# Second attention: seven of eighteen key tiles in float32, the other eleven split from PSUM, and row maxima of two heads at a time

## Chip, cores and metric

The kernel runs on one core of a Trainium2 chip. The metric is the device time of one execution in microseconds (us), median of three runs.

## What is computed

Two transformer blocks run one after the other on 2048 tokens of width 1024. The first has latent attention and a state space part. The second has attention with shared keys beside retention, then a mixture of 32 experts. Only the attention of the second block is touched. Cut to what matters it is

```python
def _attend(q, k, v):          # q (2048, 8 heads, 64); k, v (256 + 2048 keys, 2 heads, 64)
    scale = HEAD_DIM ** -0.5
    def one_block(q_blk):      # 128 queries; four query heads share a key head
        s = jnp.einsum('bqhgd,bkhd->bhgqk', q_blk, k) * scale
        p = jax.nn.softmax(s, axis=-1)
        return jnp.einsum('bhgqk,bkhd->bqhgd', p, v)
```

All inputs and outputs are float32. There are 2304 keys, 18 tiles of 128.

## The kernel before

The program is written with a framework that adds the waits and that may also shift an instruction ahead of others on its engine where operands are late. The source order is the order of first preference. Every large product uses operands of the type `float32r` (R in the code), the high and low parts of a split number; a plain float32 operand is F.

`phase_b` (L1630) makes projections. For each tile of tokens its `do_kv` (L1710) writes the keys' high and low parts to memory (k.k2), and splits the values in two: ACT casts (L318), DVE subtracts (L319), and SP stores the pair in k.v2 (L1719).

`Attention2` (L1092) works in 32 units, each of 128 queries of the four heads that share keys. `run` (L1270) is one loop over 32 x 18 steps, one key tile per step, and the parts of neighbouring units overlap in it:

- `load_q` (L1141) loads the queries of the next unit on SP's queue: q (high and low parts of a head on 128 partitions, L1146), and qm (the high parts and room for one row, L1148).
- `top` (L1151) finds the row maxima of the next unit: for each head five products pa of 512 (the last 256) keys on PE (L1161), each followed by a maximum on DVE (L1162). A last maximum (L1165), four transposes and an ACT scaling (L1173) put the negatives in row 64 of qm. The tuple `TOP` says how many of these pieces are taken in each of the 18 steps; what is left over is taken at the start of the next unit.
- `scores` (L1176): two products (L1182, L1183) give the scores of a tile less the maximum, keys on partitions, in one of two PSUM banks of the pool pS.
- `exps` (L1185): ACT takes the exponential into SBUF (p, L1187) and casts it to its high part (ph, L1191).
- `rest` (L1193): the low part pl = p - ph, on DVE for even tiles and on POOL for odd ones (L1199). High parts of the odd tiles below 17 are added up on DVE (accD, L1209); `fold` (L1214) splits the sum (L318, L319).
- `values` (L1223), five steps later: o += both parts of the values times ph (L1232); o1 += (ones, high parts of the values) times pl (L1234, L1238); and for the tiles marked E, and for the two parts of the folded sum, a product with one column of ones (L1236).
- `finish` (L1240) reads o and o1, divides by the sums and stores.
- At the steps `SIDE` (1, 9, 11, 15) one piece of retention is put in (L970 to L1087). Each takes a PSUM bank from `bank()`, of which there are two, and leaves one to some ten instructions on PE, DVE, ACT and POOL. Within a step, ACT, the maxima and the subtractions come in this order:

```python
            if n < N:
                self.exps(us[n], t)
            for _ in range(self.TOP[t]):
                next(ahead, None)
            if 0 < i <= N * NK:
                self.rest(us[(i - 1) // NK], (i - 1) % NK)
            if t in self.SIDE:
                next(self.side, None)
```

PSUM's eight banks are pA 2 (pa), pS 2 (scores), pO 2 (o, o1), pT 2.

Of the kernel before, what the change touches and what calls it, by code (L numbers as in the profile page):

```python
# [10 lines left out]
F = mybir.dt.float32  # L11
R = mybir.dt.float32r
# [3 lines left out]
OP = mybir.AluOpType  # L16
# [17 lines left out]
class K:  # L34
    """What every part of the kernel shares: the core, the arguments, constants, small helpers."""
# [27 lines left out]
    def tr(self, out, x):  # L63
        """out = x transposed, bit for bit."""
        self.nc.tensor.transpose(out, x, self.ident)  # L65

    def rsqrt(self, out, src, n):
        """out = (src / n + eps) ** -0.5 on small tiles."""
        nc = self.nc
        nc.vector.tensor_scalar(out, src, 1.0 / n, EPS, op0=OP.mult, op1=OP.add)  # L70
        w = out.free_size()
        nc.gpsimd.tensor_tensor(out, out, self.mhalf[: out.partition_size(), :w], op=OP.pow)  # L72

    def reduce_angle(self, x, k):
        """x -> x - 2 pi round(x / 2 pi), within [-pi, pi]; k: room of x's shape."""
# [8 lines left out]
    def sin_cos(self, pool, s, c, x, shape):  # L84
        """s, c = sin(x), cos(x); x is spent."""
# [8 lines left out]
    def cmul(self, pool, ore, oim, are, aim, bre, bim, shape, neg_im=False, second=None):  # L94
        """(ore + i oim) = a b, elementwise; with neg_im, oim = -Im(a b)."""
# [16 lines left out]
# Chunks of 16 tokens. Lanes of the tables: (direction, state). A table of powers has 17 entries e:  # L112
# lambda^e forward, lambda^(16 - e) backward.
# [3 lines left out]
def early(k):  # L117
    """What rests on the parameters alone, in small parts."""
# [56 lines left out]
        # Powers 0..16, ascending for both directions: [lanes, e, g].  # L175
# [16 lines left out]
        # Bbar = (lambda_bar - 1) / lambda B  # L192
# [18 lines left out]
        # Tables with e in the direction's order; pw: lambda^s' forward, lambda^(15 - s') backward.  # L211
# [10 lines left out]
        # Bbar with columns (direction, h), zero off its direction.  # L222
# [10 lines left out]
        # The skip weights, on the diagonal of lag 0: rows 32 j + h of a batch of two groups.  # L233
# [72 lines left out]
def mm3(nc, out, lh, ll, rh, rl, start, stop):  # L306
    """out (+)= (lh + ll)^T (rh + rl) in three passes; the product of the low parts is below float32."""
# [5 lines left out]
def split(nc, hi, lo, src, eng=None):  # L313
    """src = hi + lo exactly, each of 12 bits."""
# [13 lines left out]
class Proj:  # L328
    """Rows of a normalized matrix, transposed and split, against weights that stream through."""
# [18 lines left out]
    def half_block(self):  # L348
        """Room of up to two tiles, in that of the last block's low parts."""
# [4 lines left out]
    def add_rows(self, blk, i, x):  # L354
        """Tile i of four of a block: x [128 rows, 1024]."""
# [8 lines left out]
    def weights(self, c0, n, w=None, upto=8):  # L364
        """Columns of the weights, split; w: the rows that are there already."""
# [12 lines left out]
    def rows(self, blk, i, w, n):  # L378
        """PSUM [128 rows of tile i, n]."""
# [6 lines left out]
    def cols(self, blk, w, m):  # L386
        """PSUM [128 columns of weight tile m, 512 rows]."""
# [7 lines left out]
def norm_rows(k, pool, out, x, g, n, b=None):  # L395
    """out = x / rms(x) * g (+ b) over n columns."""
# [73 lines left out]
def rope_tables_1(k):  # L470
    """[c, s, (cos, cos)] and [c, s, (-sin, sin)] of 32 frequencies, to memory. Yields after each small part."""
# [140 lines left out]
class Attention:  # L612
    """For each head and 128 queries: scores with the queries on partitions, their maximum, the
    exponentials, their transposes split in two; for 256 queries the products with the values
    (stationary). The parts of neighbouring tiles of queries alternate as `order` says."""
# [25 lines left out]
    def start(self, n):  # L641
        """The tile n of queries and what it holds."""
# [20 lines left out]
    def M(self, t, j):  # L663
        """The scores times -scale, in place, and the running minimum."""
# [43 lines left out]
    def D(self, t, g, copy=None):  # L708
        """A group that stays whole, for products in float32."""
# [6 lines left out]
    def Y(self, t, g):  # L716
        """Split from the copy: the high part here, the low part on the engine that has time."""
# [6 lines left out]
    def P(self, b):  # L724
        """A share of a block's products with the values."""
# [22 lines left out]
    def X(self, b):  # L748
        """One over the sums, on all partitions."""
# [39 lines left out]
class Attention1(Attention):  # L789
# [11 lines left out]
        # The next phase's loads go to the room of the even heads, which is free first.  # L801
# [9 lines left out]
    def load_part(self, h, c):  # L811
        """One of eight parts of a head's keys and values, if it isn't there yet."""
# [87 lines left out]
        # log of the decays: -log(1 + exp(-x)), as min(x, 0) - log(1 + exp(-|x|)).  # L900
# [12 lines left out]
        # Distances on partitions: p + 1, 128 - p, 127 - p, p; and 255 - p, 127 - p, p, 128 + p.  # L913
# [5 lines left out]
        # Factors [128, head, direction]: of the queries; of the keys, with 1/8; of the context's keys.  # L919
# [7 lines left out]
        # Over a chunk, on the state's partitions (direction, dk).  # L927
# [4 lines left out]
        # Decays of the scores [key j, head, query i], with 1/8.  # L932
# [20 lines left out]
class Retention:  # L953
    def constants(self, k, cp):
        """Tables of the decays."""
        self.k = k
        k.rsb = k.scratch("rsb", [NT, 64, 512])        # states of the backward direction before each chunk
        k.ruf = k.scratch("ruf", [NT, 64, 512])        # what each chunk adds to the forward state
# [3 lines left out]
    def spread(self, wk, x, j, name):  # L962
        """[row, head, direction, 64]: x [row, (head, 64)] times factor j."""
# [128 lines left out]
class Attention2:  # L1092
# [92 lines left out]
    def exps(self, u, t):  # L1185
# [4 lines left out]
        if self.HI[t] == "A":  # L1190
            self.nc.scalar.copy(hi, p)  # L1191
# [1287 lines left out]
```

## Time and profile before

| | |
|---|---|
| median of 3 runs | 4474.56 us (4474.19 to 4477.1) |
| profiled execution, first to last instruction (span) | 4460.7 us |
| mean granted TensorE clock | 0.962 |
| second attention, first to last score product (L1183) | 2130.1 to 3185.6 us, 32 units |

The page gives no other time of the profiled execution than its span; the median of the runs is 13.9 us above it. In the profile, PE is the matmul engine and PEld its weight loads, DVE, ACT and POOL the vector, scalar and GpSimd engines, SP the queue that issues most transfers. The end of a matmul's record is modelled, and records of neighbouring matmuls overlap; what a matmul costs in a stream is read from the distance of starts. A float32 (F) matmul leaves two records, a float32r matmul one.

### The profile page before, as it was taken

The page shows a single profiled execution, that of the slowest core. Times are in us where ns is not written, and L with a number is a line of the kernel's source. Part 1 is how long each engine was busy: PE and PEld are TensorE (multiplying, and loading weights), DVE is VectorE, ACT ScalarE, POOL GpSimd, SP SyncE. Part 2 cuts the span into 40 slices and gives each one's busy share as a digit, 9 for nine tenths or more (in the row PEclk, how much of TensorE's full clock was granted, in tenths as well). Part 3 has the DMA queues.
Part 4 walks back from the last instruction along what each step waited for, and adds up shares of the span by engine and source line. Part 5 has one row for each costly group of instructions (what it writes and reads, how often), then busy time and mean ns, then how long its engine had stood idle before and what let it go on. Part 6 is the DMA issues. An engine that isn't in the chain of part 4 may idle for free. (4 is left out here: it accounts for less than half of the span.)

```text
span 4460.7 us, 60030 instructions
## 1 busy us (share of the span) xinstructions
PE 4063.1 (91%) x19842; PEld 3214.7 (72%) x19842; DVE 3244.0 (73%) x5326; ACT 2301.0 (52%) x4166; POOL 1988.3 (45%) x2239
## 2 busy tenths in 40 slices
PE   7999889999988989999888888989898799999997
PEld 5777768888876878887666666666587677777775
DVE  7563368887625365534999999999765778888886
ACT  3233455555524343322667777777521556666664
POOL 3430078882003422222555555555300566666664
PEclk9999989999998999999999999999999899999998
DMA  5543852331253464334421111110352788888885
GB/s 142 169 146 109 280 192 74 92 112 53 66 160 123 132 206 127 121 103 135 117 71 52 50 45 43 50 41 25 96 172 95 265 279 280 284 280 275 277 282 184
DMA packets 432999, 647.63 MB, mean 145 GB/s; under 512 B 88576, under 2 KB 228096, under 8 KB 432428
## 3 DMA queue, kind: packets, MB, share of 16 engines
q1 hardware_dynamic: 403868, 562.67, 39.9%
q0 software_dynamic: 21840, 66.25, 4.2%
q10 hardware_dynamic: 6976, 14.85, 1.0%
q8 instruction: 157, 2.57, 0.2%
q14 instruction: 158, 1.29, 0.1%
HBM read 496.33 MB, written 156.10 MB: 146 GB/s over the span
## 5 line engine op out<-in xcount | busy, mean ns | idle before, releaser
L1199 POOL TENSOR_TENSOR pl<-p,ph 128x512 fp32r<-128x512 f32 x288 | 416.1, 1450 | 244.8 <-ACT ph L1191 189.4
L2251 DVE TENSOR_TENSOR wlo<-raw,whi 128x1024 fp32r<-128x1024 f32 x256 | 471.6, 1855 | 66.1 <-ACT whi L2248 66.0
L2248 ACT CAST whi<-raw 128x1024 fp32r<-128x1024 f32 x384 | 394.9, 1048 | 130.9 <-DMA raw<-in_moe_w_up 43.9
L1162 DVE TENSOR_REDUCE nm<-pa 128x1 f32<-128x512 f32 (+1 forms) x640 | 390.0, 623 | 19.7 <-PE pa L1161 18.4
L1187 ACT ACTIVATE p<-ps 128x512 f32<-128x512 f32 x576 | 333.2, 599 | 105.6 <-PE ps L1183 87.0
L1161 PE MATMUL pa<-kk,q 128*128 128x512 f32 (+1 forms) x640 | 266.3, 425 | 95.7 <-DVE nm L1162 85.1
L1191 ACT CAST ph<-p 128x512 fp32r<-128x512 f32 x576 | 342.6, 624 | 7.7
L2251 POOL TENSOR_TENSOR wlo<-raw,whi 128x1024 fp32r<-128x1024 f32 x128 | 319.6, 2504 | 53.5 <-ACT whi L2248 47.4
L310 PE MATMUL z<-wh,hlo 128*128 128x512 f32 (+2 forms) x816 | 304.7, 374 | 0.0
L308 PE MATMUL z<-wh,hhi 128*128 128x512 f32 (+2 forms) x768 | 291.4, 381 | 7.5 <-DVE zo L455 2.4
L309 PE MATMUL z<-wl,hhi 128*128 128x512 f32 (+2 forms) x768 | 289.4, 377 | 2.7 <-DVE wl L319 2.7
L72 POOL TENSOR_TENSOR nr<-nr,mhalf 128x1 f32<-128x1 f32 x98 | 61.7, 631 | 499.2 <-DVE nr L70 441.1
L1199 DVE TENSOR_TENSOR pl<-p,ph 128x512 fp32r<-128x512 f32 x288 | 275.4, 956 | 9.8 <-ACT ph L1191 8.3
L1161 PEld LDWEIGHTS pa<-kk,q 128*128 128x128 f32 x640 | 124.0, 195 | 198.4 <-DVE nm L1162 167.0
L1182 PE MATMUL ps<-q,kk 128*128 128x512 f32 x576 | 241.5, 420 | 0.3
L661 PE MATMUL s<-kn,q 128*128 128x512 f32 x768 | 230.0, 407 | 10.0 <-ACT p L674 5.7
L1238 PE MATMUL o<-pl,v 128*128 128x512 f32 x544 | 220.4, 409 | 17.3 <-DVE pl L1199 12.6
L1232 PE MATMUL o<-ph,v 128*128 128x512 f32 x576 | 233.0, 407 | 2.7 <-DVE oc L1249 2.5
L1183 PE MATMUL ps<-qm,kl 65*128 65x512 f32 x576 | 229.0, 407 | 0.2
L1209 DVE TENSOR_TENSOR accD<-accD,ph 128x512 f32<-128x512 f32 x192 | 224.7, 1170 | 0.3
L693 ACT CAST ph<-pt 128x512 fp32r<-128x512 f32 x256 | 142.8, 596 | 151.1 <-PE pt L65 147.8
L697 DVE TENSOR_TENSOR pl<-pt,ph 128x512 fp32r<-128x512 f32 x256 | 167.9, 685 | 67.4 <-ACT ph L693 66.8
(634 smaller groups left out, 11924.5 us busy)
## 6 DMA issues: line engine op xcount, KB each, us to landing
raw<-in_moe_w_gate SPq DMA_DIRECT2D x128, 512.0 KB
raw<-in_moe_w_up SPq DMA_DIRECT2D x128, 512.0 KB
raw<-in_moe_w_down SPq DMA_DIRECT2D x128, 512.0 KB
raw<-in_w_in SPq DMA_DIRECT2D x136, 256.0 KB
w<-in_w_ada SPq DMA_DIRECT2D x96, 256.0 KB
xt<-in_x SPq DMA_DIRECT2D x32, 512.0 KB
xt<-x SPq DMA_DIRECT2D x28, 512.0 KB
rv<-rv SPq DMA_DIRECT2D x34, 256.0 KB
```

The lines of the kernel that those rows point to most:

```text
L308: nc.tensor.matmul(out, lh, rh, start=start, stop=False)
L309: nc.tensor.matmul(out, lh, rl, start=False, stop=False)
L310: return nc.tensor.matmul(out, ll, rh, start=False, stop=stop)
L1161: nc.tensor.matmul(pa[:, :c1 - c0], q[:, h], kk[:, c0:c1], start=True, stop=True)
L1162: nc.vector.tensor_reduce(nm[:, h, c:c + 1], pa[:, :c1 - c0], axis=AX.X, op=OP.max)
L1182: nc.tensor.matmul(ps, kk[:, ts], q, start=True, stop=False)
L1187: self.nc.scalar.activation(p, u["s"].pop(t), AF.Exp, scale=self.scale)
L1191: self.nc.scalar.copy(hi, p)
L1199: (nc.vector if self.LO[t] == "D" else nc.gpsimd).tensor_tensor(lo, p, hi.bitcast(F), op=OP.subtract)
L1232: nc.tensor.matmul(u["o"], v[:, t, 64:], hi, start=first, stop=last)
L2248: nc.scalar.copy(hi, raw)
L2251: i = eng.tensor_tensor(lo, raw, hi.bitcast(F), op=OP.subtract)
```

## The change

The 18 key tiles of the second attention are put in two lists. For the seven in WHOLE2 the exponentials stay float32 (p in SBUF) and are multiplied, as one float32 matmul, with float32 (ones, values). For the eleven in SPLIT2 the exponential is written back over the scores in PSUM, ACT casts its high part from there, and DVE alone subtracts there. POOL adds up the high parts of all eleven; one float32 matmul with a matrix whose first column is one adds that sum to o1. The products with a column of ones, `fold` and its split are gone.

The maxima come from the queries' high parts alone (before, high plus low) times the keys' high parts: two heads at a time, the one on rows 0 to 63 of the array, the other on rows 64 to 127, in two banks, then two maxima. Their queries are a third copy, qt, loaded by two more transfers. `TOP` holds 13 pieces where there are 12 (before 21 where there were 22). The score banks are three instead of two, the transposes' bank is one instead of two.

```diff
+WHOLE2 = (2, 4, 7, 9, 12, 14, 17)
+SPLIT2 = tuple(t for t in range(NT + 2) if t not in WHOLE2)
...
-    TOP = (1, 1, 1, 1, 2, 1, 1, 1, 2, 1, 1, 1, 2, 1, 1, 1, 1, 1)
+    TOP = (1, 0, 1, 1, 0, 1, 1, 0, 1, 1, 0, 1, 1, 0, 1, 1, 1, 1)
-    LO = "DPDPDPDPDPDPDPDPDP"
-    ACC = "EDEDEDEDEDEDEDEDEE"
...
-        self.pS = ctx.enter_context(k.pool("a2s", 2, space=PSUM))
+        self.pS = ctx.enter_context(k.pool("a2s", 3, space=PSUM))
-        self.pT = ctx.enter_context(k.pool("a2t", 2, space=PSUM))
+        self.pT = ctx.enter_context(k.pool("a2t", 1, space=PSUM))
-        self.ones = cp.tile([128, 1], R, name="on1")
-        nc.vector.tensor_copy(self.ones, k.ones[:, 0:1])
+        self.one = cp.tile([128, 128], F, name="on1")
+        nc.vector.memset(self.one, 0.0)
+        nc.vector.memset(self.one[:, 0:1], 1.0)
...
-            v = cp.tile([128, self.NK, 192], R, name=f"v{g}")
+            v = cp.tile([128, len(SPLIT2), 192], R, name=f"v{g}")
+            vw = cp.tile([128, len(WHOLE2), 128], F, name=f"vw{g}")
...
+            nc.sync.dma_start(vw[:, :, 64:], k.v2w[g].rearrange("t p n -> p t n"))
...
     def load_q(self, n):
...
+        qt = self.qp.tile([128, 2, 128], R, name="qt")
+        for i in range(2):
+            self.nc.sync.dma_start(qt[64 * i:64 * i + 64].bitcast(F), src[0:64, i::2])
...
     def top(self, n):
-        for h in range(4):
+        for j in range(2):
             for c in range(5):
                 c0, c1 = c * 512, min(c * 512 + 512, self.NK * 128)
-                pa = self.pA.tile([128, 512], F, name="pa")
-                nc.tensor.matmul(pa[:, :c1 - c0], q[:, h], kk[:, c0:c1], start=True, stop=True)
-                nc.vector.tensor_reduce(nm[:, h, c:c + 1], pa[:, :c1 - c0], axis=AX.X, op=OP.max)
+                pa = [self.pA.tile([128, 512], F, name="pa") for _ in range(2)]
+                for i in range(2):
+                    r = slice(64 * i, 64 * i + 64)
+                    nc.tensor.matmul(pa[i][:, :c1 - c0], qt[r, j], kk[r, c0:c1], start=True, stop=True)
+                for i in range(2):
+                    nc.vector.tensor_reduce(nm[:, 2 * j + i, c:c + 1], pa[i][:, :c1 - c0], axis=AX.X, op=OP.max)
                 yield
...
     def exps(self, u, t):
+        ps = u["s"].pop(t)
+        if t in WHOLE2:
+            u["p"][t] = p = self.wk.tile([128, 512], F, name="p", bufs=5)
+            self.nc.scalar.activation(p, ps, AF.Exp, scale=self.scale)
+            return
+        self.nc.scalar.activation(ps, ps, AF.Exp, scale=self.scale)
+        hi = self.wk.tile([128, 512], R, name="ph", bufs=self.RING)
+        self.nc.scalar.copy(hi, ps)
...
     def rest(self, u, t):
+        if t in WHOLE2:
+            return
         lo = self.wk.tile([128, 512], R, name="pl", bufs=self.RING)
-        (nc.vector if self.LO[t] == "D" else nc.gpsimd).tensor_tensor(lo, p, hi.bitcast(F), op=OP.subtract)
+        nc.vector.tensor_tensor(lo, ps, hi.bitcast(F), op=OP.subtract)
...
+            nc.gpsimd.tensor_tensor(acc, u["acc"], hi.bitcast(F), op=OP.add)
...
     def values(self, u, t):
-        for x in ([hi] if self.ACC[t] == "E" else []) + (u["sum"] if last and "sum" in u else []):
-            nc.tensor.matmul(u["o1"][0:1], self.ones, x, start=False, stop=False)
+        if last:
+            nc.tensor.matmul(u["o1"], self.one, u["acc"], start=False, stop=False)
+        if t in WHOLE2:
+            nc.tensor.matmul(u["o1"], vw[:, WHOLE2.index(t)], p, start=False, stop=last)
+        else:
+            nc.tensor.matmul(u["o"], v[:, j, 64:], hi, start=first, stop=t == SPLIT2[-1])
+            nc.tensor.matmul(u["o1"], v[:, j, 0:128], lo, start=first, stop=last)
...
         def do_kv(z, s):
+            if kt in WHOLE2:
+                vw = wk.tile([128, 2, 64], F, name="vt")
+                nc.scalar.copy(vw, v)
+                nc.sync.dma_start(k.v2w[:, WHOLE2.index(kt)].rearrange("h p n -> p h n"), vw)
```

## Rows read from the trace of the kernel before

**Rows 1.** The page's engines: busy time, share of the span, instructions

```profile
PE 4063.1 (91%) x19842; PEld 3214.7 (72%) x19842; DVE 3244.0 (73%) x5326; ACT 2301.0 (52%) x4166; POOL 1988.3 (45%) x2239
```

**Rows 2.** Windows of first attention, projections, second attention: length, engines, clock, DMA

```profile
core 0: us, PE busy (x) PEld busy (x) DVE busy (x) ACT busy (x) POOL busy (x), PEclk, DMA share, GB/s
640.00:1250.00 610.00, 603.80 (x3778) 520.53 (x3777) 486.26 (x1061) 330.09 (x828) 352.09 (x866) 1.00 0.26 77
1620.00:2108.00 488.00, 471.38 (x2401) 390.39 (x2402) 248.35 (x505) 166.81 (x338) 107.70 (x166) 0.99 0.41 130
2143.00:3151.00 1008.00, 897.84 (x3969) 627.74 (x3968) 985.30 (x1583) 735.57 (x1371) 561.67 (x393) 0.97 0.19 51
```

**Rows 3.** Waits in 2143 to 3150 us: us in total, times, longest

```profile
PEld pa L1161 <- DVE nm L1162: 155.1, 195, 4.2
PE pa L1161 <- DVE nm L1162: 81.2, 87, 3.8
PE pa L1161 <- DMA q<-q: 3.9, 7, 1.7
```

**Rows 4.** Line L1183, weight loads and matmuls: ns min/median/max, first and last start

```profile
L1183 PEld LDWEIGHTS ps<-qm,kl x576: 186/188/334, 2130.0 to 3185.4; 65*128 65x128 f32 x192
L1183 PE MATMUL ps<-qm,kl x576: 387/396/774, 2130.1 to 3185.6; 65*128 65x512 f32 x192
```

**Rows 5.** Instruction groups of DVE and ACT in 2143 to 3150 us

```profile
L1162 DVE TENSOR_REDUCE nm<-pa 128x1 f32<-128x512 f32 x483 | 325.0, 676 | 10.7 <-PE pa L1161 10.1
L1191 ACT CAST ph<-p 128x512 fp32r<-128x512 f32 x545 | 324.6, 624 | 7.5
L1187 ACT ACTIVATE p<-ps 128x512 f32<-128x512 f32 x544 | 314.7, 599 | 93.0 <-PE ps L1183 77.2 <-POOL pl L1199 8.0 <-PE pa L1161 2.4
L1199 DVE TENSOR_TENSOR pl<-p,ph 128x512 fp32r<-128x512 f32 x272 | 256.8, 944 | 7.8 <-ACT ph L1191 6.5
L1209 DVE TENSOR_TENSOR accD<-accD,ph 128x512 f32<-128x512 f32 x181 | 208.6, 1153 | 0.3
L1076 DVE TENSOR_SCALAR on<-on,mv,r 128x128 f32<-128x128 f32 x64 | 51.2, 850 | 1.6 <-POOL r L72 1.6
L1162 DVE TENSOR_REDUCE nm<-pa 128x1 f32<-128x256 f32 x120 | 49.0, 408 | 0.3
L1209 DVE TENSOR_TENSOR accD<-ph 128x512 f32<-128x512 f32 x30 | 31.7, 1056 | 0.0
L319 DVE TENSOR_TENSOR suml<-accD,sumh 128x512 fp32r<-128x512 f32 x30 | 21.1, 703 | 0.0
L319 DVE TENSOR_TENSOR wol<-raw,woh 128x1024 fp32r<-128x1024 f32 x1 | 1.2, 1212 | 0.0
```

**Rows 6.** Timeline of PE, second attention: start us, length of the record

```profile
2166.28 0.40 PE L1236 MATMUL o<-ph,on 128*1 128x512 f32 x1
2166.51 0.40 PE L1236 MATMUL o<-sumh,on 128*1 128x512 f32 x1
...
2167.69 0.52 PE L1161 MATMUL pa<-kk,q 128*128 128x256 f32 x2
2168.05 0.39 PE L1182 MATMUL ps<-q,kk 128*128 128x512 f32 x1
```

**Rows 7.** Timeline of a retention piece on PE; two instruction groups of retention

```profile
2610.02 0.39 PE L1060 MATMUL pt<-rv,sm 128*128 128x128 f32 x2
2610.24 0.39 PE L1061 MATMUL pt<-rst,qxt 128*128 128x128 f32 x2
...
L1061 PE MATMUL pt<-rst,qxt 128*128 128x128 f32 x128 | 24.7, 274 | 0.0
L65 PE MATMUL pt<-ident,on 128*128 128x128 f32 x64 | 12.9, 304 | 1.6 <-DVE on L1076 1.6
```

**Rows 8.** Subtractions of the two attentions by line: ns min/median/max, first and last start

```profile
L697 DVE TENSOR_TENSOR pl<-pt,ph x256: 671/683/693, 643.0 to 1259.0; 128x512 fp32r<-128x512 f32 x128
L1199 DVE TENSOR_TENSOR pl<-p,ph x288: 669/692/2964, 2133.5 to 3187.2; 128x512 fp32r<-128x512 f32 x144
L1199 POOL TENSOR_TENSOR pl<-p,ph x288: 1253/1314/2086, 2137.5 to 3188.3; 128x512 fp32r<-128x512 f32 x144
```

**Rows 9.** Float32 matmuls: timeline of PE (256 columns), line L1569 (512 columns)

```profile
1259.08 1.03 PE L1394 MATMUL pz<-tz,ut 128*128 128x256 f32 x4
1259.95 0.59 PE L1396 MATMUL pz<-o,st 128*128 128x256 f32 x2
...
L1569 PE MATMUL pz<-acc,ones x32: 590/590/591, 681.0 to 1101.3; 128*1 128x512 f32 x32
```

**Rows 10.** Timeline of loads and of PE where a unit begins

```profile
2596.47 0.55 SPq L1146 DMA_DIRECT2D q<-q  x1
2597.10 0.60 SPq L1148 DMA_DIRECT2D qm<-q  x1
...
2599.69 0.79 PE L1161 MATMUL pa<-kk,q 128*128 128x512 f32 x1 [0.39 <-DMA q<-q]
```

More of the change, by code (lines that the diff above doesn't have):

```diff
@@ L1134, in __init__ @@
             nc.sync.dma_start(v[:, :, 64:].bitcast(F), k.v2[g].rearrange("t p n -> p t n"))
-            nc.gpsimd.tensor_copy(v[:, :, 0:64], k.ones[:, None, 0:64].to_broadcast([128, self.NK, 64]))
-            self.kv.append((kk, kl, v))
+            nc.sync.dma_start(vw[:, :, 64:], k.v2w[g].rearrange("t p n -> p t n"))
+            nc.gpsimd.tensor_copy(v[:, :, 0:64], k.ones[:, None, 0:64].to_broadcast([128, len(SPLIT2), 64]))
+            nc.gpsimd.tensor_copy(vw[:, :, 0:64], k.ones[:, None, 0:64].to_broadcast([128, len(WHOLE2), 64]))
+            self.kv.append((kk, kl, v, vw))
     def bank(self):
@@ L1178, in scores @@
         kk, kl = self.kv[u["n"] % 2][:2]
-        q, qm = (x.rearrange("p h n -> p (h n)") for x in self.q[u["n"]])
+        q, qm = (x.rearrange("p h n -> p (h n)") for x in self.q[u["n"]][:2])
         ts = slice(t * 128, t * 128 + 128)
@@ L1185, in exps @@
     def exps(self, u, t):
-        p = self.wk.tile([128, 512], F, name="p", bufs=5)
-        self.nc.scalar.activation(p, u["s"].pop(t), AF.Exp, scale=self.scale)
+        ps = u["s"].pop(t)
[4 more added lines that the diff above has]
+        self.nc.scalar.activation(ps, ps, AF.Exp, scale=self.scale)
         hi = self.wk.tile([128, 512], R, name="ph", bufs=self.RING)
-        u["p"][t] = [p, hi]
-        if self.HI[t] == "A":
-            self.nc.scalar.copy(hi, p)
+        self.nc.scalar.copy(hi, ps)
+        u["p"][t] = ps, hi
     def rest(self, u, t):
         nc = self.nc
-        p, hi = u["p"][t]
-        if self.HI[t] == "D":
-            nc.vector.tensor_copy(hi, p)
+        if t in WHOLE2:
+            return
+        ps, hi = u["p"][t]
         lo = self.wk.tile([128, 512], R, name="pl", bufs=self.RING)
-        (nc.vector if self.LO[t] == "D" else nc.gpsimd).tensor_tensor(lo, p, hi.bitcast(F), op=OP.subtract)
+        nc.vector.tensor_tensor(lo, ps, hi.bitcast(F), op=OP.subtract)
         u["p"][t] = hi, lo
-        e = self.ACC[t]
-        if e in "DP":
-            eng = nc.vector if e == "D" else nc.gpsimd
-            had = u["acc"].get(e)
-            if had is None:
-                u["acc"][e] = hi.bitcast(F), False
-            else:
-                acc = had[0] if had[1] else self.wk.tile([128, 512], F, name="acc" + e, bufs=1)
-                eng.tensor_tensor(acc, had[0], hi.bitcast(F), op=OP.add)
-                u["acc"][e] = acc, True
-            if t == max(self.ACC.rfind(x) for x in "DP"):
-                self.fold(u)
-    def fold(self, u):
-        nc = self.nc
-        accs = [x[0] for x in u["acc"].values()]
-        for x in accs[1:]:
-            nc.vector.tensor_tensor(accs[0], accs[0], x, op=OP.add)
-        u["sum"] = [self.wk.tile([128, 512], R, name="sum" + n, bufs=1) for n in "hl"]
-        split(nc, *u["sum"], accs[0])
+        if t == SPLIT2[0]:
+            u["acc"] = hi.bitcast(F)
+        else:
+            acc = u["acc"] if t > SPLIT2[1] else self.wk.tile([128, 512], F, name="acc")
+            nc.gpsimd.tensor_tensor(acc, u["acc"], hi.bitcast(F), op=OP.add)
+            u["acc"] = acc
     def values(self, u, t):
@@ L1229, in values @@
             u["o1"] = self.pO.tile([128, 512], F, name="o1")
-        v = self.kv[u["n"] % 2][2]
-        hi, lo = u["p"].pop(t)
-        nc.tensor.matmul(u["o"], v[:, t, 64:], hi, start=first, stop=last)
-        if first:
-            nc.tensor.matmul(u["o1"], v[:, t, 0:128], lo, start=True, stop=False)
-        for x in ([hi] if self.ACC[t] == "E" else []) + (u["sum"] if last and "sum" in u else []):
-            nc.tensor.matmul(u["o1"][0:1], self.ones, x, start=False, stop=False)
-        if not first:
-            nc.tensor.matmul(u["o1"], v[:, t, 0:128], lo, start=False, stop=last)
+        v, vw = self.kv[u["n"] % 2][2:]
+        p = u["p"].pop(t)
+        if last:
+            nc.tensor.matmul(u["o1"], self.one, u["acc"], start=False, stop=False)
+        if t in WHOLE2:
+            nc.tensor.matmul(u["o1"], vw[:, WHOLE2.index(t)], p, start=False, stop=last)
+        else:
+            hi, lo = p
+            j = SPLIT2.index(t)
+            nc.tensor.matmul(u["o"], v[:, j, 64:], hi, start=first, stop=t == SPLIT2[-1])
+            nc.tensor.matmul(u["o1"], v[:, j, 0:128], lo, start=first, stop=last)
     def finish(self, u):
@@ L1278, in run @@
                 if t == 0:
[L1279 removed]
+                    us[n] = dict(n=n, p={}, s={})
                     for _ in ahead:
@@ L1715, in do_kv @@
             kt = (s + 2) % (NT + 2)
-            vt = wk.tile([128, 2, 2, 64], R, name="vt")
             v = z[:, 128:256].rearrange("p (n c) -> p n c", c=64)
-            split(nc, vt[:, :, 0], vt[:, :, 1], v)
-            nc.sync.dma_start(k.v2[:, kt].rearrange("h p n -> p h n"), vt.bitcast(F).rearrange("p h a n -> p h (a n)"))
+            if kt in WHOLE2:
+                vw = wk.tile([128, 2, 64], F, name="vt")
+                nc.scalar.copy(vw, v)
+                nc.sync.dma_start(k.v2w[:, WHOLE2.index(kt)].rearrange("h p n -> p h n"), vw)
+            else:
+                vt = wk.tile([128, 2, 2, 64], R, name="vt")
+                split(nc, vt[:, :, 0], vt[:, :, 1], v)
+                nc.sync.dma_start(k.v2[:, SPLIT2.index(kt)].rearrange("h p n -> p h n"),
+                                  vt.bitcast(F).rearrange("p h a n -> p h (a n)"))
             def late():
```

15 lines of the change are left out of this document (5 added, 10 removed).

## The prediction

> **What bounds the kernel now.** The page's engine line comes first [rows 1]: PE is busy for 91% of the span, and that number misleads, since records of neighbouring matmuls overlap. The change touches one stage, so the windows come next [rows 2]. In 1008 us of the second attention DVE is busy for 985.3 us (98%); PE's records cover 898, ACT 736, POOL 562. The waits agree [rows 3]: PE stands for 155.1 + 81.2 us until DVE has taken a maximum (L1162) and given a bank of pa back. So DVE sets the pace. The score products run from 2130.1 to 3185.6 us [rows 4]: 33.0 us for each of 32 units. The window holds 544 exponentials [rows 5], 544 / 18 = 30.2 units.
>
> What PE could do is read from starts. Six products of 512 columns start from 2166.28 to 2167.69 (four in lines left out), so 1.41 / 6 = 0.235 us each; the two of 256 behind them need 0.36 together [rows 6]. Retention's 128-column records follow each other in 0.11 [rows 7]. Retention has some 720 of them, four groups such as L1061 and four of transposes, the longest shown [rows 7]: 22 a unit. A unit has 16 + 36 + 36 + 12 = 100 products of 512 columns and four of 256, and with retention and four transposes of the maxima it needs 23.5 + 0.7 + 2.4 + 0.45 = 27.1 us of 33.0. PE has 6 us to spare, no more.
>
> **DVE, the part that binds.** Sums over the window [rows 5]: maxima 325.0 + 49.0, subtractions 256.8, additions 208.6 + 31.7, the split of the sum 21.1, and twelve smaller groups, from L1076 (51.2) to a weight split (1.2), 185.4 together: 1077.6, or 35.7 us a unit, in 32.6 us of busy time, as records overlap a little. The change keeps the maxima (12.4 a unit) and the small groups (6.1). The additions (8.0) and the split (0.7) go. Nine subtractions from SBUF (8.5) become eleven from PSUM. Their price is that of L697, the same operation with the same shape from PSUM: 0.683, never over 0.693, though POOL was busy for 352 of 610 us there [rows 2, 8]; from SBUF beside POOL the line reaches 2.964 [rows 8]. So 11 x 0.683 = 7.5. New sum 26.0, or 23.8 with the same overlap: 8.8 us a unit come off the engine that binds.
>
> **PE, which is late next.** Removed: twelve products with one column, 12 x 0.235 = 2.8. Scores (36) and the products of eleven split tiles (22) stay at 58 x 0.235 = 13.6. Fourteen products of the whole tiles become seven float32 matmuls, and the sum of the high parts is an eighth. Their price: a float32 matmul leaves two records; two of 256 columns take 0.87 us from start to start [rows 9], and 512 columns have a record of 0.590 [rows 9] against 0.40 for float32r [rows 6], which fits twice as long a stream in each of the two. So 0.87 each, 8 x 0.87 = 7.0, against 14 x 0.235 = 3.3: this part of the change makes PE's work longer.
>
> The pairs of maxima are in no row. Lower bound: both halves run at once, 0.235 a pair (0.18 for the short ones): 2.2 a unit. Upper bound from the same operation: one after the other, 0.47 (0.36), 4.5. A further cost of changing between whole array and halves is a rival below. With no row nearer than the plain product, I take halfway, 3.3. Then PE needs 13.6 + 7.0 + 3.3 + 2.4 + 0.45 = 26.8 us (25.7 to 28.0), and at the granted clock of the window, 0.97 [rows 2], 27.6. So PE takes the place of DVE, some 5 us below today's unit.
>
> **Waits that come.** Eleven of eighteen score banks are now given back by DVE instead of ACT. Three banks last three steps of about 1.6 us, 4.9; score products, exponential, cast and subtraction take 0.64 + 0.60 + 0.62 + 0.68 = 2.5 of it [rows 5, 6, 8]. A pair of maxima (1.35) fits into the 2.4 that are left; a piece of retention such as the four L1076 (4 x 0.85 = 3.4) [rows 5] doesn't, and then PE stands with scores, values and maxima queued behind it. The two transfers of qt stand behind q and qm on SP. SP started q at 2596.47 and qm at 2597.10, and the first maximum waited for q until 2599.69 [rows 10]; such waits of PE come to 3.9 us in the window [rows 3]. Two more issues of about 0.6 make it 1.2 to 1.8 us later, once a unit, hidden where other products are put first. Against this the transposes of a maximum now end inside the unit (12 pieces in 13 places), where one was left over. One bank for transposes instead of two can hold a piece of retention up. I book 2 us a unit for all of them, between 0.5 and 5. Sum: 27.6 + 2 = 29.6 us a unit.
>
> **What costs nothing.** ACT loses seven casts and the sum's cast: 24.4 us a unit falls by 7 x 0.62 + 0.62 = 5.0 [rows 2, 5]; should exponentials into PSUM be a tenth of a microsecond dearer, ACT still has ten to spare. POOL has 18.6 us a unit [rows 2] and trades nine subtractions for ten additions, one more of 1.31 [rows 8]; its sum is wanted five steps after the last split tile. If POOL runs late, the eighth float32 product waits. In the projections seven subtractions of the values go and seven stores are half as long; PE covers 471 of 488 us there [rows 2].
>
> **Sum.** 33.0 - 29.6 = 3.4 us, times 32: 109 us. The profiled span of 4460.7 falls to 4352; the median lies 13.9 above the span, so 4474.6 - 109 = 4365.
>
> **The rivals.**
> *Changing the array's shape costs more than the pairs save (slower).* Ten pairs make twenty changes a unit. A record lasts 0.40 while the next begins after 0.235 [rows 6]: if the array has to be emptied at each change, 0.165 is lost, and if the next weights can't be loaded meanwhile, about 0.19 more, a weight load's record [rows 4], 0.35 x 20 = 7.1. PE is then 25.7 + 7.1 = 32.8, at 0.97 33.8, with 2 of waits 35.8: +2.8 x 32 = +90, 4565. At 0.165 alone it gives 29.0 / 0.97 + 2 = 31.9, that is 4439. It decides from the point where PE takes 33.0 less 2 of waits: (31.0 x 0.97 - 25.7) / 20 = 0.22 us a change. The profile shows no matmul on half of the rows in this stage, so nothing speaks for it but the thin margin of PE; against it, the 65-row products stand among 128-row ones without a gap [rows 4, 6], though those are not halves.
> The Trainium skill's "TensorEngine Tiling (Array Packing)", section Tiling Modes, says that a change of the tiling mode drains the engine, while two row tiles may double the rate. No row before shows either. By that rule the sum is 4439 if a drain is what the modelled record shows, and 4565 if the weights wait too; by the rows alone it is 4365.
>
> *The pairs run in turn (the change doesn't do what it says).* DVE gives the two banks back 0.68 apart, and other products may slip in between. PE 28.0 / 0.97 + 2 = 30.9: -2.1 x 32 = -67, 4407.
>
> *The score banks become the wait.* Four pieces of retention a unit, each 0.6 over the slack, and the late qt at 1.8: 4.4 us of waits, 27.6 + 4.4 = 32.0: -32, 4443. For it speaks that today's DVE queue is full; against it, that the change empties a quarter of it.
>
> *Nearly all of it (faster than forecast).* Pairs at once, waits 1.0: 25.7 / 0.97 + 1.0 = 27.5: -5.5 x 32 = -176, 4299.
>
> **How the numbers follow.** Forecast 0.42 (4330 to 4395); pairs in turn 0.15; score banks 0.12; nearly all 0.12; changes of shape 0.14; the terms cancel to within 9 us 0.05. Faster 0.42 + 0.15 + 0.12 + 0.12 = 0.81, same 0.05, slower 0.14; 0.2% (9 us) is about what a measurement can tell here. The range takes in the first three, most of "nearly all", no change and the mildest of the slower case: 4280 to 4490.
>
> **What would show it.** Right: L1209, `fold` and the products with one column gone, subtractions at 0.68, DVE at some 80% of the window, unit length 28 to 31, and PE the engine others wait for, with float32 records two by two 0.43 apart. Pairs at once show as two pa records that start together, in turn as starts 0.235 apart. A gap before and after each pair shows the rival that is slower. Waits of score products for DVE's subtraction show the banks, waits of pa for a transfer the late qt. The prediction is wrong if a unit stays above 32 us.

## The result and the profile after

The changed kernel takes 4407.93 us (median of 4 runs, 4406.94 to 4412.52) against 4475.83 us for the kernel before in the same runs (4474.19 to 4482.13): 67.9 us less, a ratio of 0.9845 with a 95% interval of 0.9831 to 0.9859. The profiled execution has a span of 4410.8 us, 2.9 above its median. The spans of the two profiled executions differ by 49.9 only, since the one of before lay 13.9 under its median; stages are therefore compared, not spans.

First the page's engines, then the window of the second attention (columns as in [rows 2]), then two lines of it by tile (ns min/median/max, first and last start):

```profile
PE 4121.2 (93%) x19522; PEld 3145.3 (71%) x19522; DVE 2952.2 (67%) x5128; ACT 2170.6 (49%) x3910; POOL 1948.6 (44%) x2273
```

```profile
2150.00:3090.00 940.00, 935.30 (x3655) 548.78 (x3654) 710.50 (x1397) 609.49 (x1124) 524.99 (x423) 1.00 0.22 58
```

```profile
L1193 PE MATMUL ps<-qm,kl x576: 390/397/803, 2136.5 to 3124.4; 65*128 65x512 f32 x192
L1212 DVE TENSOR_TENSOR pl<-ps,ph x352: 648/681/693, 2143.6 to 3125.3; 128x512 fp32r<-128x512 f32 x176
```

L1193 is the score product that [rows 4] show as L1183. Its starts spanned 1055.5 us and now span 987.9: 67.6 us less, as much as the medians differ. The rest of the program took 3405.2 us in the profiled execution before and 3422.8 after; over the eleven profiled executions of this study it lies between 3405 and 3427, and no run tells whether the change has a part in that. A unit went from 33.0 to 987.9 / 32 = 30.87 us. In the window DVE fell from 98% [rows 2] to 710.5 / 940 = 76%, and PE rose from 89% to 99.5%. The bound has moved from DVE to PE, and PE hardly ever stands any more. Four rows of the waits say the same (us in total, times, longest us):

```profile
ACT ps L1201 <- PE ps L1193: 187.3, 180, 2.3
DVE nm L1175 <- PE pa L1173: 113.9, 182, 2.1
PEld pa L1173 <- DVE nm L1175: 64.1, 112, 1.1
PE ps L1192 <- DVE pl L1212: 1.4, 1, 1.4
```

In [rows 3] PE waited for DVE. Now ACT and DVE wait for PE's products. The 64.1 us stand on weight loads, which run ahead of the matmuls; of PE's own matmuls the row of L1192 is the longest wait in the window. The groups of the same window (columns as in [rows 5]) show what the other engines gained:

```profile
L1219 POOL TENSOR_TENSOR acc<-acc,ph 128x512 f32<-128x512 f32 x273 | 348.0, 1275 | 225.9 <-ACT ph L1203 217.3 <-DMA rk<-rk 2.0 <-PE o L1240 1.8
L1175 DVE TENSOR_REDUCE nm<-pa 128x1 f32<-128x512 f32 x480 | 311.2, 685 | 104.0 <-PE pa L1173 101.3
L1212 DVE TENSOR_TENSOR pl<-ps,ph 128x512 fp32r<-128x512 f32 x333 | 225.1, 683 | 82.7 <-ACT ph L1203 81.6
L1201 ACT ACTIVATE ps<-ps 128x512 f32<-128x512 f32 x332 | 193.6, 587 | 190.4 <-PE ps L1193 187.3 <-DVE nm L1175 1.0 <-ACT p L1199 1.0
L1173 PE MATMUL pa<-kk,qt 64*128 64x512 f32 x480 | 140.9, 497 | 1.0 <-DVE nm L1175 0.6
L1076 DVE TENSOR_SCALAR on<-on,mv,r 128x128 f32<-128x128 f32 x64 | 25.5, 459 | 7.8 <-POOL r L72 7.8
```

The record of a maximum (L1173) is 497 ns long, against 0.40 us for other products of 512 columns. What such a pair really costs PE is read from starts, in the timeline of PE (start us, length of the record):

```profile
2615.37 0.40 PE L1239 MATMUL o<-ph,v 128*128 128x512 f32 x1
2615.61 0.39 PE L1240 MATMUL o<-pl,v 128*128 128x512 f32 x1
2615.93 0.49 PE L1173 MATMUL pa<-kk,qt 64*128 64x512 f32 x2
2616.35 0.50 PE L1192 MATMUL ps<-q,kk 128*128 128x512 f32 x1
2616.69 0.40 PE L1193 MATMUL ps<-qm,kl 65*128 65x512 f32 x1
2616.92 0.40 PE L1239 MATMUL o<-ph,v 128*128 128x512 f32 x1
2617.16 0.40 PE L1240 MATMUL o<-pl,v 128*128 128x512 f32 x1
2617.48 0.49 PE L1173 MATMUL pa<-kk,qt 64*128 64x512 f32 x1
2617.91 0.50 PE L1192 MATMUL ps<-q,kk 128*128 128x512 f32 x1
2618.34 0.50 PE L1173 MATMUL pa<-kk,qt 64*128 64x512 f32 x1
2618.77 0.50 PE L1193 MATMUL ps<-qm,kl 65*128 65x512 f32 x1
2619.11 1.02 PE L1233 MATMUL o<-acc,on 128*128 128x512 f32 x2
2619.97 1.02 PE L1235 MATMUL o<-p,vw 128*128 128x512 f32 x2
...
2637.24 0.38 PE L1173 MATMUL pa<-kk,qt 64*128 64x256 f32 x2
2637.55 0.50 PE L1192 MATMUL ps<-q,kk 128*128 128x512 f32 x1
```

Three things are to be seen. Plain products still follow each other in 0.23 to 0.24 (2615.37 to 2615.61). A float32 product takes 0.86 (2619.11 to 2619.97). And the two maxima of a pair share one row with x2 and one length of 0.49: they run at once. But the pair begins 0.32 after the product before it instead of 0.235, the product behind it begins 0.42 later, and the one behind that 0.34 later. From 2615.61 to 2616.69 the pair and two plain products take 1.08, so the pair costs 1.08 - 2 x 0.235 = 0.61 us, more than the 0.47 that two products over all rows take. At 2617.48 a pair is torn apart by a score product: from 2617.16 to 2619.11 are 1.95, and less three plain products that pair costs 1.24. With 256 columns the next product begins 0.31 after the pair (2637.24 to 2637.55) instead of 0.42, which makes 0.50 for such a pair together and, with both halves shorter, 1.01 torn. In the window 203 pairs of 512 columns are together, with nothing between their halves, and 37 torn; of the 60 pairs of 256 columns 24 and 36. In 218 of the 227 that are together the halves start 3 to 4 ns apart. Over the 203 the medians of the three distances are 0.33, 0.43 and 0.34, so the pair read above is a usual one.

### The profile page after: what moved, and what is told of

Its sections match the earlier page's. It is cut to its first block, busy times and chain, and to the rows that moved or that the text cites. A ratio compares the mean times of both kernels' runs of the same rounds, so it can differ in the third digit from the quotient of the medians.

```text
span 4410.8 us, 58986 instructions
## 1 busy us (share of the span) xinstructions
PE 4121.2 (93%) x19522; PEld 3145.3 (71%) x19522; DVE 2952.2 (67%) x5128; ACT 2170.6 (49%) x3910; POOL 1948.6 (44%) x2273
## 5 line engine op out<-in xcount | busy, mean ns | idle before, releaser
L1219 POOL TENSOR_TENSOR acc<-acc,ph 128x512 f32<-128x512 f32 x288 | 367.2, 1275 | 235.0 <-ACT ph L1203 226.0
L1201 ACT ACTIVATE ps<-ps 128x512 f32<-128x512 f32 x352 | 205.2, 587 | 200.1 <-PE ps L1193 196.9
L1212 DVE TENSOR_TENSOR pl<-ps,ph 128x512 fp32r<-128x512 f32 x352 | 238.1, 683 | 96.8 <-ACT ph L1203 95.7
L1192 PE MATMUL ps<-q,kk 128*128 128x512 f32 x576 | 299.6, 521 | 2.2 <-DVE pl L1212 1.4
L1193 PE MATMUL ps<-qm,kl 65*128 65x512 f32 x576 | 237.8, 414 | 0.8
L1235 PE MATMUL o<-p,vw 128*128 128x512 f32 x448 | 230.1, 594 | 0.0
L1203 ACT CAST ph<-ps 128x512 fp32r<-128x512 f32 x352 | 204.9, 588 | 22.6 <-DMA mx<-oc 1.5
L739 PE MATMUL o<-ph,v 128*128 128x256 f32 x1024 | 215.7, 292 | 0.2 <-ACT ph L693 0.2
L1173 PEld LDWEIGHTS pa<-kk,qt 64*128 64x128 f32 x640 | 78.9, 186 | 189.9 <-DVE nm L1175 77.8
L1173 PE MATMUL pa<-kk,qt 64*128 64x512 f32 (+1 forms) x640 | 199.1, 483 | 5.2 <-DMA kk<-k 3.1
L674 ACT ACTIVATE p<-s,nm 128x512 f32<-128x512 f32 x256 | 177.2, 708 | 8.6 <-DVE s L666 8.6
```

The costliest lines, as they stand in the source:

```text
L1173: nc.tensor.matmul(pa[i][:, :c1 - c0], qt[r, j], kk[r, c0:c1], start=True, stop=True)
L1192: nc.tensor.matmul(ps, kk[:, ts], q, start=True, stop=False)
L1193: nc.tensor.matmul(ps, kl[:, ts], qm, start=False, stop=True)
L1212: nc.vector.tensor_tensor(lo, ps, hi.bitcast(F), op=OP.subtract)
L1219: nc.gpsimd.tensor_tensor(acc, u["acc"], hi.bitcast(F), op=OP.add)
```

## The experiments

All were timed in rounds with the kernel before on the same chip (medians of 4473.8 to 4475.99 there, single runs of it from 4452.89 to 4491.77). The change itself was timed in another round, so differences to it lean on these medians. A unit is the span of the starts of the second score product, divided by 32.

| run | edit | us, median | ratio to before, 95% | unit, us |
|---|---|---|---|---|
| the change | | 4407.93 | 0.9845 (0.9831 to 0.9859) | 30.87 |
| e1_whole_rows | change, maxima on all rows | 4338.13 | 0.9696 (0.9672 to 0.9721) | 28.81 |
| e2_halves_only | before, maxima on halves | 4530.72 | 1.0134 (1.009 to 1.0178) | 34.42 |
| e3_same_half | change, both heads on one half | 4479.96 | 1.0008 (0.999 to 1.0025) | 33.16 |
| e4_two_banks | change, two score banks | 4441.1 | 0.992 (0.9896 to 0.9945) | 31.72 |
| g_one_tile | change, a pair in one tile | 4391.85 | 0.9818 (0.9791 to 0.9846) | 30.29 |
| f_whole5 | e1, 5 float32 tiles | 4343.59 | 0.97 (0.9679 to 0.9721) | 29.05 |
| f_whole3 | e1, 3 float32 tiles | 4393.6 | 0.9818 (0.9795 to 0.9841) | 30.57 |
| f5_late_q | f_whole5, maxima begin later | 4344.16 | 0.9703 (0.9681 to 0.9726) | 28.95 |
| h_whole7_late_q | e1, maxima begin later | 4344.12 | 0.9704 (0.9678 to 0.973) | 29.21 |

### The change without the halves: e1_whole_rows

```diff
-        return q, qm, qt
+        return q, qm
...
-                    r = slice(64 * i, 64 * i + 64)
-                    nc.tensor.matmul(pa[i][:, :c1 - c0], qt[r, j], kk[r, c0:c1], start=True, stop=True)
+                    nc.tensor.matmul(pa[i][:, :c1 - c0], q[:, 2 * j + i], kk[:, c0:c1], start=True, stop=True)
```

qt and its two transfers are gone; the float32 tiles, the split from PSUM and the places of the maxima stay.

> The changed kernel, but each head's maxima come from one product on all 128 rows of the array, as before the change (queries' high and low parts, keys' high parts), and qt is not loaded. Theory A (a change between whole array and halves costs about 0.09 us on the way in and 0.10 on the way out, and a quarter of the pairs pays both twice): the maxima fall from some 7.4 us of TensorE a unit to 4.5 at most, a unit from 30.9 to some 28.2, the time by 60 to 95 us against the changed kernel, to 4315 to 4350. Theory B (halves that run at once save what two products cost): the unit becomes 2 us longer, about 4475.

Measured: 4338.13 us, 69.8 below the change. The halves made the change worse, and the rest of it is worth 4474.35 - 4338.13 = 136 us. That qt isn't loaded is hardly the reason: no maximum of the change waits for a load, and e3_same_half below, which doesn't load qt either, is slower than the change by what its pairs cost. The window, two waits and the score product of this kernel (columns as above):

```profile
2150.00:3050.00 900.00, 883.05 (x3743) 618.92 (x3743) 714.12 (x1423) 619.33 (x1157) 541.42 (x435) 1.00 0.21 57
```

```profile
PEld pa L1169 <- DVE nm L1171: 55.6, 149, 1.5
PEld pa L1169 <- DMA q<-q: 20.5, 29, 2.6
```

```profile
L1189 PE MATMUL ps<-qm,kl x576: 391/395/800, 2133.4 to 3055.5; 65*128 65x512 f32 x192
```

PE is still the busiest, at 98%, but 17 of 900 us are now without a record, and weight loads wait for q (20.5 us in the window, of which 4.7 reach the matmuls). The maxima are 16 x 0.235 + 4 x 0.18 = 4.5 us of PE's unit here; with 13.6 + 6.9 + 2.4 + 0.45 for the rest that makes 27.85, and 1.9% idle time brings it to 28.4, against 28.81 measured.

### The halves alone on the kernel before: e2_halves_only

```diff
-    TOP = (1, 1, 1, 1, 2, 1, 1, 1, 2, 1, 1, 1, 2, 1, 1, 1, 1, 1)
+    TOP = (1, 0, 1, 1, 0, 1, 1, 0, 1, 1, 0, 1, 1, 0, 1, 1, 1, 1)
...
+        qt = self.qp.tile([128, 2, 128], R, name="qt")
+        for i in range(2):
+            self.nc.sync.dma_start(qt[64 * i:64 * i + 64].bitcast(F), src[0:64, i::2])
...
-                nc.tensor.matmul(pa[:, :c1 - c0], q[:, h], kk[:, c0:c1], start=True, stop=True)
+                for i in range(2):
+                    r = slice(64 * i, 64 * i + 64)
+                    nc.tensor.matmul(pa[i][:, :c1 - c0], qt[r, j], kk[r, c0:c1], start=True, stop=True)
...
-        p = self.wk.tile([128, 512], F, name="p", bufs=5)
+        p = self.wk.tile([128, 512], F, name="p", bufs=4)
```

The last edit makes room for qt; it is a second, small change that this run can't tell from the first.

> The kernel before, with the maxima on the array's halves and nothing else of the change (one buffer less for p, to make room for qt). Theory A (VectorE set the pace before, and the halves only make TensorE's work longer, 27.1 to about 30 us of 33.0): within 15 us of the kernel before, or slower; above 4465. Theory B (the halves carry the gain): at least 40 us faster than before.

Measured: 4530.72 us, 56 above the kernel before. The window and a stretch of PE's timeline:

```profile
2150.00:3050.00 900.00, 873.72 (x3402) 509.73 (x3401) 812.03 (x1357) 624.68 (x1169) 476.97 (x337) 0.99 0.21 56
```

```profile
2500.83 0.40 PE L1242 MATMUL o<-ph,on 128*1 128x512 f32 x1
2501.16 0.50 PE L1166 MATMUL pa<-kk,qt 64*128 64x512 f32 x1
2501.59 0.50 PE L1244 MATMUL o<-pl,v 128*128 128x512 f32 x1
2502.01 0.50 PE L1166 MATMUL pa<-kk,qt 64*128 64x512 f32 x1
2502.44 0.50 PE L1188 MATMUL ps<-q,kk 128*128 128x512 f32 x1
2502.78 0.40 PE L1189 MATMUL ps<-qm,kl 65*128 65x512 f32 x1
```

DVE went from 98% to 90% of the window and PE from 89% to 97%: the halves alone make PE the bound of a kernel in which it had 6 us of each unit to spare. The timeline shows why. Here the order of PE's instructions puts other products between the halves of most pairs, so that each half has the array to itself for 0.43. In the window only 40 of 255 pairs are together. At the prices read above (0.61 and 1.24 for 512 columns, 1.01 for a torn pair of 256) the maxima take 11.0 us a unit; with them PE's 27.1 of before becomes 27.1 - 4.5 + 11.0 = 33.6, and with the 2.9% of idle time 34.6, against 34.42 measured. The sum leaves nothing that the missing buffer of p would have to explain.

### Do the halves overlap at all? e3_same_half

```diff
-                    nc.tensor.matmul(pa[i][:, :c1 - c0], qt[r, j], kk[r, c0:c1], start=True, stop=True)
+                    nc.tensor.matmul(pa[i][:, :c1 - c0], qm[0:64, 2 * j + i], kk[0:64, c0:c1], start=True, stop=True)
```

Both heads of a pair use rows 0 to 63, so they can only follow each other; qt isn't loaded.

> The changed kernel, but both heads of a pair use rows 0 to 63 of the array (the high parts in qm, the keys' rows 0 to 63), so the two can't run at once; qt is not loaded. Theory A (the pairs do run at once, and what eats the gain is the change of shape): the second product of a pair adds some 0.21 us, 10 pairs a unit, 32 units: 50 to 70 us slower than the changed kernel, 4458 to 4478. Theory B (the pairs ran in turn all along): no difference, 4400 to 4415.

Measured: 4479.96 us (10 runs, 4468.1 to 4492.27), 72 above the change, two above the range of theory A, and no gain over the kernel before. PE's timeline:

```profile
2600.28 0.73 PE L1169 MATMUL pa<-kk,qm 64*128 64x512 f32 x2
2600.94 0.50 PE L1188 MATMUL ps<-q,kk 128*128 128x512 f32 x1
2601.27 0.40 PE L1189 MATMUL ps<-qm,kl 65*128 65x512 f32 x1
```

The next product begins 0.66 after the pair's start, where it was 0.42 with two halves: 0.24 later, one product's time. A unit of this kernel has 6.1 pairs of 512 columns together and 1.9 torn, and of the short ones 0.64 and 1.36. With 0.24 more for each that is together (0.12 for a short one) the maxima take 9.3 us by the prices above (0.85, 1.24, 0.62, 1.01) where the change has 7.25: 2.1 of the 2.29 by which the unit is longer, and the greater part of it is the 0.24. In the change, then, the two halves of a pair that is together do run at once. So the rival "the pairs run in turn" is false as a mechanism; that its time, 4407, is the one measured is chance.

### Keeping pairs together: g_one_tile

```diff
-        self.pA = ctx.enter_context(k.pool("a2a", 2, space=PSUM))
+        self.pA = ctx.enter_context(k.pool("a2a", 1, space=PSUM))
...
-                pa = [self.pA.tile([128, 512], F, name="pa") for _ in range(2)]
+                pp = self.pA.tile([128, 2, 512], F, name="pa")
+                pa = [pp[:, i] for i in range(2)]
```

With one tile for both banks the two products become free to start at the same moment.

> The changed kernel with the two banks of a pair of maxima as one PSUM tile, so that the two products become ready together; in the instruction order of TensorE some 302 of 320 pairs then stand side by side instead of some 242. Theory A (a pair torn apart pays the change of shape twice, about 0.6 us more): 60 pairs x 0.6 = up to 36 us faster than the changed kernel, 4370 to 4395, still behind e1_whole_rows. Theory B (side by side or not is the same, the cost is in each product): 4400 to 4415. If the later start of a pair makes VectorE wait, it is slower than 4415.

Measured: 4391.85 us, 16 below the change. In 2150 to 3050 us all 59 pairs of 256 columns are together and 216 of 233 of 512. By the prices above the maxima fall from 7.25 to 6.25 us a unit; of this 1.0, the unit shows 0.58, as PE's records now cover 883.5 of 900 us (98.2%) instead of 99.5%. Torn pairs are a part of the loss, but with nearly every pair together the kernel is still 54 us behind e1_whole_rows. That fits the price of a pair that is together: 6.25 against 4.5 us of maxima a unit are 56 us in 32 units.

### The third score bank: e4_two_banks

```diff
-        self.pS = ctx.enter_context(k.pool("a2s", 3, space=PSUM))
+        self.pS = ctx.enter_context(k.pool("a2s", 2, space=PSUM))
...
-        self.pT = ctx.enter_context(k.pool("a2t", 1, space=PSUM))
+        self.pT = ctx.enter_context(k.pool("a2t", 2, space=PSUM))
```

> The changed kernel with two score banks and two for transposes instead of three and one. Theory A (the third bank is what keeps VectorE's late release of scores off TensorE): 1 to 3 us a unit more, 4440 to 4505, with waits of the score products for VectorE's subtraction in the trace. Theory B (the banks don't matter, since TensorE's own work fills the unit): 4400 to 4415.

Measured: 4441.1 us, 33 above the change, at the lower end of theory A; the unit is 0.85 us longer, less than the 1 to 3 of that theory. The window of this run, and the wait that theory A names:

```profile
2150.00:3050.00 900.00, 892.30 (x3441) 512.77 (x3440) 662.77 (x1320) 562.45 (x1053) 488.58 (x395) 1.00 0.22 58
```

```profile
PEld ps L1192 <- DVE pl L1212: 29.8, 58, 1.0
PE ps L1192 <- DVE pl L1212: 4.7, 9, 0.7
```

The wait has grown: in the same 900 us of the change it is 7.2 us (16 times) on the weight loads and 1.4 on the matmuls. But PE's records still cover 99.1% of the window, which leaves 0.27 us of idle time a unit, 0.12 more than in the change. More comes from the pairs: 57 of 223 pairs of 512 columns and 35 of 55 of 256 are torn here, and by the prices above the maxima take 7.82 us a unit instead of 7.25. These 0.57 and the 0.12 are 0.69 of the 0.85. So the rival "the score banks become the wait" is a true mechanism only in small part; the greater part of what a third bank saves is that fewer pairs are torn. That the late banks are what changes the order of PE's products is argued, not shown. A longer wait for the only transpose bank did not show in the change.

### Fewer float32 tiles: f_whole5 and f_whole3

With whole rows, is PE bound so firmly that each float32 tile taken away (0.87 against 2 x 0.235 for a split tile) shortens the unit by 0.4? Both kernels are e1_whole_rows with one more line changed.

```diff
-WHOLE2 = (2, 4, 7, 9, 12, 14, 17)
+WHOLE2 = (3, 6, 10, 13, 17)
```

```diff
-WHOLE2 = (2, 4, 7, 9, 12, 14, 17)
+WHOLE2 = (5, 11, 17)
```

> The version of e1_whole_rows (maxima on all rows of the array) with five float32 tiles (3, 6, 10, 13, 17) instead of seven. Theory A (TensorE sets the pace, and a float32 tile costs it 0.87 us where a split one costs 0.47): 2 x 0.40 = 0.8 us a unit less, some 20 to 26 us faster than e1_whole_rows, 4310 to 4320. Theory B (VectorE, ACT and POOL, which get 1.4, 1.2 and 2.6 us more a unit, and the score banks are already the limit): no faster or slower, above 4330.

> As f_whole5, with three float32 tiles (5, 11, 17). Theory A, still TensorE: 4 x 0.40 = 1.6 us a unit less than e1_whole_rows, 4285 to 4295. Theory B (up to five split tiles in a row hold all three score banks, and VectorE is at some 26 us of 27): the gain stops, 4310 to 4360.

Measured: 4343.59 us (no difference from e1 that these runs can tell) and 4393.6 us (55 slower, above the ranges of both theories). The window and some waits of each, five tiles first:

```profile
2150.00:3050.00 900.00, 860.23 (x3700) 613.40 (x3699) 763.58 (x1475) 648.54 (x1199) 613.22 (x491) 0.99 0.21 57
```

```profile
PE pa L1169 <- DVE nm L1171: 17.9, 15, 3.6
PEld ps L1188 <- DVE pl L1208: 9.0, 18, 3.4
```

```profile
2150.00:3050.00 900.00, 823.68 (x3515) 587.61 (x3514) 779.31 (x1462) 641.06 (x1196) 654.32 (x522) 0.97 0.21 55
```

```profile
PEld ps L1188 <- DVE pl L1208: 30.9, 57, 3.5
PE pt L65 <- DVE on L1076: 18.9, 22, 1.0
PE pa L1169 <- DMA q<-q: 14.2, 17, 2.4
PE ps L1188 <- DVE pl L1208: 12.3, 17, 3.3
```

PE's records fall from 883 to 860 and 824 of 900 us, but no engine takes its place as a full one: DVE comes to 87% with three tiles. What PE saves turns into idle time: 0.54 us a unit with seven tiles, 1.28 with five, 2.59 with three. No single wait carries it. With three tiles PE's own matmuls wait for retention's L1076 on DVE (18.9 us), for q (14.2), for a score bank that DVE gives back late (12.3, none with seven) and for the maxima's banks (11.6). The granted clock falls as well, from 1.00 in the window of e1 to 0.99 and 0.97. With three tiles PE's 27.85 of e1 becomes 27.85 - 1.6 = 26.25; at 0.97 that is 27.1, and with 8.5% of idle time 29.6, against 30.57 measured: the last 1.0 is open. Nor does a run tell the number of float32 tiles from their places. Of the three counts tried, seven and five are level and three is worse.

### Maxima that begin one step later: f5_late_q and h_whole7_late_q

e1's wait for q (20.5 us on the weight loads) suggests to begin the maxima one step later. The same edit was put on f_whole5 and on e1.

```diff
-    TOP = (1, 0, 1, 1, 0, 1, 1, 0, 1, 1, 0, 1, 1, 0, 1, 1, 1, 1)
+    TOP = (0, 1, 1, 1, 0, 1, 1, 0, 1, 1, 0, 1, 1, 1, 1, 1, 1, 1)
```

> f_whole5 with the first piece of the maxima one step later in the unit (TOP begins with 0). Theory A (the wait of the first maximum for the load of q, 20.5 us in 900 in the trace of e1_whole_rows, holds TensorE up once a unit): 10 to 22 us faster than f_whole5. Theory B (other products fill that wait or it moves on): within 6 us of f_whole5.

> e1_whole_rows (seven float32 tiles, maxima on all rows) with the first piece of the maxima one step later. Theory A (TensorE sets the pace there and the wait for q, some 0.7 us a unit, is on its path): 8 to 22 us faster than e1_whole_rows, 4316 to 4330. Theory B (the wait moves elsewhere, as f5_late_q showed with five float32 tiles): 4332 to 4345.

Measured: 4344.16 against 4343.59, and 4344.12 against 4338.13; nothing is gained, and with seven tiles the two ranges overlap. With five tiles the waits are now:

```profile
PEld pa L1169 <- DMA q<-q: 4.7, 10, 1.1
PEld pa L1169 <- DVE nm L1171: 42.8, 53, 3.6
```

On f_whole5 the two were 19.2 and 34.5 us. Most of the wait for q goes, and the wait for DVE grows: the maxima are packed closer in the later places. With seven tiles the wait for q does not go at all: it is 25.8 us on the weight loads, where e1 has 20.5, and 9.0 instead of 4.7 on the matmuls; why, no run shows. The best kernel of the study stays e1_whole_rows, 3.0% below the kernel before and 1.6% below the change (4338.13 / 4407.93).

## Why the prediction was right, and where it was not

The prediction was right in sign and its range holds the result; the time lies 43 us above the forecast of 4365, and above 4395, where the case it gave the best chance (0.42) ends.

**DVE stops being the bound: right.** The eleven subtractions from PSUM were priced at 0.683 and take 683 ns, never over 693. DVE was put at 23.8 us a unit and has 710.5 / 940 x 30.87 = 23.3. ACT was put at 19.4 and has 20.0. POOL was put at 19.9 and has 17.2: its additions take 1275 ns where 1314 was the median of its subtraction [rows 8], and its other work got shorter too.

**The split from PSUM beside POOL: right, by the row.** Of the two prices in [rows 8], the one from PSUM held. The Trainium skill's "SBUF — State Buffer", section "Who interferes with whom", states that a VectorE instruction with two SBUF inputs contends with a GpSimd instruction that reads SBUF, and one with at most one doesn't. The trace agrees: L1199, with both inputs in SBUF, reached 2.964 us [rows 8], and L1212, with one, 0.693, beside a POOL that was busy for 525 of 940 us.

**PE takes DVE's place: right.** The float32 price of 0.87, built in the prediction from records of other shapes, measures 0.86.

**The term that was mis-sized: the pairs of maxima.** The step reads "I take halfway, 3.3", between 2.2 for halves at once and 4.5 for halves in turn. The trace gives 6.8 x 0.61 + 1.2 x 1.24 for pairs of 512 columns, together and torn, and 0.8 x 0.50 + 1.2 x 1.01 for those of 256: 7.25 us a unit. The upper bound itself was too low, since it took a half for a plain product. The 7.25 are made of three parts: 2.24 for halves at once, as in the lower bound; 3.64 for going into the halves and out of them; and 1.37 for torn pairs, which stood in no term and in no rival.

**The rival that held the cause: changes of shape, at the milder price.** It named 0.165 a change, or 0.35. Measured is 0.61 - 0.235 = 0.375 for both changes of a pair: 0.09 before the pair, 0.19 because the next product starts 0.42 to 0.43 after the pair instead of 0.235, 0.10 with the product behind that (0.34 instead of 0.235); halved, 0.19 for each of the two changes. The rival's sum at 0.165 came to 4439 and not 4407 because its errors did not quite cancel: the clock and the waits that it took on were 2.75 us a unit too dear, and it lacked 0.34 for the dearer change and 1.37 for the torn pairs. Its place in the argument was right ("the thin margin of PE"), and e2_halves_only shows its side: on the kernel before, where PE had 6 us to spare, the halves alone make the time worse.
The Trainium skill's "TensorEngine Tiling (Array Packing)", section "Tiling Modes", has both halves of this: different tiles compute in parallel, and a change of mode drains the engine. The trace agrees with the first (the halves start 3 to 4 ns apart) and shows a cost at the change, 0.42 until the next start, for which a drain may be the reason; for pairs of 512 columns this cost outweighs the gain.

**Two terms that were too dear and hid it.** The clock was taken at 0.97, as the window of before showed, and 0.8 us was added for it; the window after has 1.00. Waits were booked at 2 us; PE's records leave 4.7 of 940 us, 0.15 a unit. No maximum waits for q or qt in the change, and the score banks cost 1.4 us in the whole window. Together: 29.6 + 3.95 (pairs) - 0.8 - 1.85 - 0.1 (float32) = 30.8, measured 30.87. In time the pairs alone are worth 3.95 x 32 = 126 us above the forecast, and the two others gave 85 back. Without these two errors the forecast with the pairs' real price would have been 4365 + 126 = 4491, slower than before and just outside the range: that sign and range came out right is in part luck.

**A rival that was added up wrongly.** In "the score banks become the wait" a piece of 3.4 us lies 1.0 and not 0.6 over a slack of 2.4, four times 0.6 and 1.8 make 4.2 and not 4.4, and such pieces are rarer: the 64 records of L1076 [rows 5], four to a piece, are 16 pieces in 30.2 units and not four in each. With three banks this wait cost PE's matmuls 1.4 us in 940, so nothing in the result hangs on it.

**What the parts are worth.** Float32 tiles with the split from PSUM bring 136 us, shown by e1_whole_rows. The halves cost 56 alone and 70 on top of the other part. It stays open which part of a change of shape is the emptying and which the loading of weights: no run separates them. A run that puts several pairs in a row between two changes was not tried, as two banks of pa hold one pair.

## What to carry to other kernels

Two half-array products that run at once are a gain only if they cost less than two whole ones where they stand; here the switch in and out made a pair 0.61 us against 0.47, and each pair that the order of instructions tore apart 1.24. Before making an engine that isn't the bound do more to relieve one that is, work out what the next bound takes per unit, and give each part of a change a run of its own: one part here was worth twice the whole. When an engine is near the balance with others, work taken off it can come back as waits: here five float32 tiles were no faster than seven, and three were slower.

## What the runs showed of the hardware that was not expected

Other instructions of DVE and POOL got shorter when work left DVE. The mean of L1076 on DVE fell from 850 [rows 5] to 459 ns, and a step of POOL in finishing a unit is another, before and after:

```profile
L1254 POOL TENSOR_TENSOR oc<-oc,os 64x512 f32<-64x512 f32 x30 | 49.6, 1654 | 22.4 <-ACT os L1250 18.5 <-ACT ph L1191 1.9 <-PE o L1236 1.3
L1256 POOL TENSOR_TENSOR oc<-oc,os 64x512 f32<-64x512 f32 x30 | 38.3, 1278 | 66.8 <-ACT os L1252 66.8
```

It took 1654 ns on average in the kernel before, where DVE and POOL both had subtractions with two inputs in SBUF, and 1278 after. That their meeting is the cause is argued, not shown: no run put one of these instructions beside the other alone. An exponential from PSUM into PSUM (L1201) takes 587 ns, a little less than the 599 into SBUF [rows 5]; ACT's cast takes 589 ns from PSUM (L1203) and took 624 from SBUF [rows 5].
